# A two-layer encoder on one core: two moving operands in one 512-column matmul, and PSUM laid out anew

## The chip, the cores and the metric

The kernel runs on one core of a Trainium2 chip. The metric is the device time of one execution, in microseconds (us). Before the change three runs took 979.34, 980.66 and 981.9 us; the median is 980.66. A profile is one further execution, recorded by the hardware. Its rows name TensorE's products PE and its weight loads PEld, VectorE DVE, ScalarE ACT, GpSimd POOL and the engine that issues most transfers SP.

## What is computed

Two layers, each with three blocks on x (256 tokens by 1024, float32). The first and the third are feed-forwards, the second mixes tokens in three ways. Cut to what the change touches:

```python
def swiglu(x, w_gate, w_up, w_down):
    return (jax.nn.silu(x @ w_gate) * (x @ w_up)) @ w_down

for l in range(DEPTH):                                    # DEPTH = 2, D_FF = 2816
    x = layer_norm(ALPHA * x + 0.5 * swiglu(x, ffn1_w_gate[l], ffn1_w_up[l], ffn1_w_down[l]), ...)
    proj = x @ w_in[l]                                    # 1024 x 2560
    u, gb, gc, h, q, k, v = jnp.split(proj, splits, axis=-1)
    y_a = pool_mixer(u, pool_w[l], pool_scale[l])
    y_b = gated_conv_mixer(gb, gc, h, conv_w[l])
    y_c = neighbourhood_attention(q, k, v, rpb[l])        # 8 heads of 64
    x = layer_norm(ALPHA * x + jnp.concatenate([y_a, y_b, y_c], axis=-1) @ w_out[l], ...)
    x = layer_norm(ALPHA * x + 0.5 * swiglu(x, ffn2_w_gate[l], ffn2_w_up[l], ffn2_w_down[l]), ...)
```

## The kernel before

**Two parts of a number.** TensorE works here in a reduced float32 format (float32r). The kernel keeps precision by splitting each weight w into an upper part (whi, a cast on ScalarE, L178) and a lower part (wlo, the remainder, a subtraction on VectorE, L179), and each activation likewise: xhi and xlo (L270, L271), hT and yT with two halves. A product x w is then three matrix products: upper by upper, lower x by upper w, upper x by lower w.

**Units of weights.** All weights come in 330 units of 128 x 1024 (512 KB). `load` issues a unit's transfer on SP into one of 4 raw buffers and orders the two splits. 12 units may be live in split form. `Pacer` is a hand-written order: every group of products ends with `pc.step(us)`, which moves a planned clock on, runs the hooks that are due (work of other engines, and small TensorE jobs such as transposes, ordered with `pc.at(delay, tag, fn)`) and orders at most one further unit. `pc.need(tag)` runs the hooks of a tag at once. Each engine carries out its instructions in the order in which they were written.

**Three kinds of groups.**
- `x_stat` (L274 to L292): one tile of 128 tokens is stationary, 512 columns of weights move past; the result has tokens on its rows.
- `w_stat` (L294 to L309): 256 columns of weights are stationary, in two halves of 128 (`ft`), and all 256 tokens move past; the result comes transposed. For each half and each of the 8 chunks of 128 rows there are the three products L303, L304, L305 of 256 columns, all into one 256-column half of a bank. Two units and 48 products make a projection.
- `r_stat` (L311 to L317): activations stationary, 512 columns of weights moving, into the accumulators `acc`.

**Feed-forward.** The first four column tiles go through `x_stat`. Then, for each pair p of column tiles (2 to 10), `w_stat` makes gate; silu reads it from PSUM on ScalarE (L391); `w_stat` makes up; VectorE multiplies it by 0.5 and by silu's result into hf (L396); ScalarE and VectorE split hf into hT (L474, L475). The down projection of the pair before follows (24 products); those of the last three pairs are done in `finish`, one token tile after the other, with the layer norm, whose new x is transposed (L268) and split for the next block.

**Mixers.** v and the pair u, gb go through `x_stat`; q, k (two halves of the heads), gc and h through `w_stat`, in the order q0, k0, q1, k1, gc, h. The copies qT (L759, four with mirrored columns and the scale) and kT (L763) are read by the attention, whose steps are hooks: scores on TensorE (L686), bias and maximum on VectorE (L695, L697), exponentials on ScalarE (L700), normalisation on VectorE (L710, L712, tile pz), transposes of pz on TensorE (L721) that ScalarE copies out as PT (L726), and the products PT by v (L735, called PV below), copied out and split as yT. Two such stages (j = 0, 1) run for each half q of the heads. The pool mixer ends in a product of its own (L619, hook `ya`, 16 us on the planned clock after its means were ordered), the convolution runs on VectorE.

**PSUM** has 8 banks of 128 x 512 float32. `bank("acc")` takes one of 4 for the accumulators and the scores, `bank()` one of 4 others (tag `mm`) for everything else, in turn.

Of the kernel before, what the change touches and what calls it, by code (L numbers as in the profile page):

```python
# [9 lines left out]
F32 = mybir.dt.float32  # L10
# [50 lines left out]
# about how long a product of the tensor engine takes: these pace the work of the other engines  # L61
MM512 = 0.218
MM256 = 0.1095


class Pacer:
    """Places work of the other engines, and the next weights, between groups of matrix products."""
# [53 lines left out]
def encoder_kernel(  # L121
# [18 lines left out]
    ps_acc = ctx.enter_context(tc.tile_pool(name="ps_acc", bufs=4, space=PSUM))  # L140
    ps_mm = ctx.enter_context(tc.tile_pool(name="ps_mm", bufs=4, space=PSUM))
# [24 lines left out]
    def bank(tag="mm"):  # L166
        pool = ps_mm if tag == "mm" else ps_acc
        return pool.tile([P, 512], F32, tag=tag, name=nm(tag))

# [88 lines left out]
    def new_xT():  # L258
        hi = xp.tile([P, KC, SEQ], F32R, tag="xhi", name=nm("xhi"))
        lo = xp.tile([P, KC, SEQ], F32R, tag="xlo", name=nm("xlo"))  # L260
        return hi, lo
# [12 lines left out]
    def x_stat(ps, key, cols, t, xT, free):  # L274
        """One token tile against columns of the weights, a step per unit."""
# [18 lines left out]
    def w_stat(ps, key, xT):  # L294
        """256 columns of the weights against all tokens, transposed out."""
        for ft in range(2):
            c = slice(ft * P, (ft + 1) * P)
            for i in range(2):
                hi, lo = pc.get((*key, i))
                for j in range(4):  # L300
                    kc = i * 4 + j
                    o = ps[:, ft * SEQ : (ft + 1) * SEQ]
                    PE.matmul(o, hi[:, j, c], xT[0][:, kc, :], start=(kc == 0), stop=False)  # L303
                    PE.matmul(o, hi[:, j, c], xT[1][:, kc, :], start=False, stop=False)  # L304
                    PE.matmul(o, lo[:, j, c], xT[0][:, kc, :], start=False, stop=(kc == KC - 1))  # L305
                if ft == 1:
                    pc.free((*key, i))
                if ft == 0 or i == 0:
                    pc.step(12 * MM256)  # L309

    def r_stat(ps, key, act, t, n, first, last):  # L311
        """A chunk of transposed activations against half a row unit."""
# [86 lines left out]
    def ffn(key, xT, next_gb, stop, store=False):  # L399
# [17 lines left out]
        # first four column tiles with the token tiles apart  # L417
        gk, uk = (*key, "g", 0), (*key, "u", 0)
        if key == (0, 0):
# [9 lines left out]
            for k in (gk, uk):  # L429
                ps = [bank() for _ in range(NT)]  # L430
# [16 lines left out]
        else:  # L447
            for t in range(NT):
                pc.need(f"x{t}")
                gate = bank()  # L450
# [3 lines left out]
                up = bank()  # L454
# [10 lines left out]
        for p in range(2, NPAIR):  # L465
            gate = bank()
            w_stat(gate, (*key, "g", p), xT)
            sg = silu(gate)
            pc.step(12 * MM256)
            up = bank()  # L470
# [3 lines left out]
            ACT.copy(hT[:, 0], hf)  # L474
            DVE.tensor_tensor(hT[:, 1], hf, f32(hT[:, 0]), ALU.subtract)  # L475
            pc.step(12 * MM256)
            pc.need("h")
            # the down projection runs behind
# [15 lines left out]
    consts = {}  # L494

    def setup():
# [8 lines left out]
        # additive mask of a query column block: its rows run with the column falling  # L505
# [38 lines left out]
        pc.at(30, "cw", columns)  # L544
        # the bias table, each line in the middle of a longer one
# [12 lines left out]
        # probabilities: the columns out of a block's reach stay zero  # L558
# [26 lines left out]
    def mixers(l, xT, next_gb, stop):  # L585
# [12 lines left out]
        biases = {0: load_bias(l, 0)}  # L598

# [30 lines left out]
        for t in range(NT):  # L630
            pc.need(f"x{t}")
            pv = bank()
# [3 lines left out]
            pu = bank()  # L636
# [16 lines left out]
        def proj(name):  # L653
            ps = bank()
            w_stat(ps, (*key, name), xT)
            return ps.rearrange("p (a b) -> p a b", a=2)
# [13 lines left out]
        def attention(j, qT, kT, q):  # L670
            """Two heads, in the upper and the lower half of the rows: one stage after the other."""
# [174 lines left out]
```

## Time and profile before

| | |
|---|---|
| median of three runs (lowest, highest) | 980.66 us (979.34, 981.9) |
| profiled execution, from its first to its last instruction | 979.4 us |
| TensorE products | 6201, 4032 of them L303 to L305 |
| weight casts L178, weight splits L179 | 321 each, 1045 and 1231 ns |
| HBM read | 176.84 MB, 182 GB/s over the span |
| mean granted clock of TensorE | 0.991 |

The profile has only the span of the profiled execution; what lies before its first and after its last instruction isn't in it. A page of the profile gives shares of busy time, a chain that is followed back from the last instruction, and groups of instructions (line, engine, operation, written tile <- read tiles, shapes, count; then busy us, mean ns of one; then the engine's idle time before them and what ended it). A timeline gives start and duration of each instruction in us. Products are pipelined: a product's duration overlaps that of the next one.

### The profile page before, as it was taken

To read this page: it belongs to the slowest core of one execution; us is meant where nothing else is said; L and a number is where in the kernel's file an instruction comes from. 1 tells how busy PE (TensorE), PEld (TensorE's weight loads), DVE (VectorE), ACT (ScalarE), POOL (GpSimd) and SP (SyncE) were. 2 spreads that over 40 slices of the span, in tenths; PEclk is the share of its full clock that TensorE was granted. 3 is DMA by queue.
4 is the path that set the end of the run, shared out by engine and by line. 5 is a ranking of instruction groups with operands and counts; after the bars stand their busy time and mean duration, and the time that the engine had idled before them with its cause. 6 is when DMAs were issued, how large, how long until landed. Compare 5 with 4: busy or idle time off the path is not lost.

```text
span 979.4 us, 15259 instructions
## 1 busy us (share of the span) xinstructions
PE 950.6 (97%) x6201; PEld 865.1 (88%) x6201; DVE 580.3 (59%) x670; ACT 437.7 (45%) x585; POOL 65.6 (7%) x118
## 2 busy tenths in 40 slices
PE   7999999998999999999999999999889999999996
PEld 5999999878888999999888999998688889999995
DVE  5755544676768644545676454548676776454525
ACT  6544434335734534434344444443465354344410
POOL 4000000024101000000000000002050000000001
PEclk9999999999999999999999999999989999999999
DMA  8887665568345866565468556664754377556601
GB/s 287 277 264 216 190 194 173 145 185 241 106 129 169 258 194 188 175 195 177 135 211 254 176 172 194 191 186 110 252 153 123 109 229 243 177 174 193 192 23 43
DMA packets 129077, 178.95 MB, mean 183 GB/s; under 512 B 14752, under 2 KB 100848, under 8 KB 129008
## 3 DMA queue, kind: packets, MB, share of 16 engines
q1 hardware_dynamic: 129008, 177.99, 59.3%
q8 instruction: 48, 0.79, 0.3%
q14 instruction: 21, 0.17, 0.0%
HBM read 176.84 MB, written 1.13 MB: 182 GB/s over the span
## 4 chain that ended last, share of the span: by engine, by line
PE 83%; DVE 7%; DMA 5%; issue 2%; ACT 1%; POOL 1%; SPq 1%; POOLq 0%; DVEq 0%; ACTq 0%
PE mm L303 16%; PE mm L304 16%; PE mm L305 16%; PE acc L315 9%; PE acc L316 9%; PE acc L317 9%; DMA raw<-in_w_in_dram 3%; DVE wlo L179 2%; PE mm L292 2%; PE mm L290 2%; PE mm L291 2%; ACT whi L178 1%; PE mm L721 1%; DMA raw<-in_ffn_w_down_dram 1%; DMA raw<-in_ffn_w_up_dram 1%
## 5 line engine op out<-in xcount | busy, mean ns | idle before, releaser
L179 DVE TENSOR_TENSOR wlo<-raw,whi 128x1024 fp32r<-128x1024 f32 (+1 forms) x321 | 390.0, 1231 | 303.1 <-ACT whi L178 302.0
L178 ACT CAST whi<-raw 128x1024 fp32r<-128x1024 f32 (+1 forms) x321 | 331.1, 1045 | 328.9 <-issue 131.2
L303 PE MATMUL mm<-xhi,whi 128*128 128x256 f32 x1344 | 384.0, 286 | 0.0
L304 PE MATMUL mm<-xlo,whi 128*128 128x256 f32 x1344 | 382.0, 284 | 0.0
L305 PE MATMUL mm<-xhi,wlo 128*128 128x256 f32 x1344 | 381.8, 284 | 0.0
L303 PEld LDWEIGHTS mm<-xhi,whi 128*128 128x128 f32 x1344 | 259.7, 193 | 3.0 <-issue 1.5
L304 PEld LDWEIGHTS mm<-xlo,whi 128*128 128x128 f32 x1344 | 259.6, 193 | 1.4
L305 PEld LDWEIGHTS mm<-xhi,wlo 128*128 128x128 f32 x1344 | 259.5, 193 | 0.0
L315 PE MATMUL acc<-whi,hT 128*128 128x512 f32 x352 | 137.9, 392 | 0.0
L316 PE MATMUL acc<-whi,hT 128*128 128x512 f32 x352 | 137.4, 390 | 0.0
L317 PE MATMUL acc<-wlo,hT 128*128 128x512 f32 x352 | 137.0, 389 | 0.0
L317 PEld LDWEIGHTS acc<-wlo,hT 128*128 128x128 f32 x352 | 66.1, 188 | 14.0
L291 PE MATMUL mm<-whi,xlo 128*128 128x512 f32 x192 | 75.3, 392 | 2.9 <-DVE xlo L271 2.9
L315 PEld LDWEIGHTS acc<-whi,hT 128*128 128x128 f32 x352 | 66.2, 188 | 12.7
L316 PEld LDWEIGHTS acc<-whi,hT 128*128 128x128 f32 x352 | 66.2, 188 | 12.3
L290 PE MATMUL mm<-whi,xhi 128*128 128x512 f32 x192 | 76.7, 399 | 0.4 <-ACT whi L178 0.4
L292 PE MATMUL mm<-wlo,xhi 128*128 128x512 f32 x192 | 75.2, 392 | 0.5 <-DVE wlo L179 0.5
L342 POOL TENSOR_SCALAR rs<-mv 128x1 f32<-128x1 f32 x12 | 9.4, 780 | 847.0 <-DVE mv L341 847.0
L474 ACT CAST hT<-hf 128x512 fp32r<-128x512 f32 x36 | 22.3, 620 | 75.2 <-DVE hf L396 75.2
L291 PEld LDWEIGHTS mm<-whi,xlo 128*128 128x128 f32 x192 | 36.4, 189 | 10.8 <-DVE xlo L271 3.8
L292 PEld LDWEIGHTS mm<-wlo,xhi 128*128 128x128 f32 x192 | 36.2, 188 | 8.9 <-DVE wlo L179 1.3
L290 PEld LDWEIGHTS mm<-whi,xhi 128*128 128x128 f32 x192 | 36.3, 189 | 8.2 <-ACT whi L178 1.3
(93 smaller groups left out, 556.9 us busy)
## 6 DMA issues: line engine op xcount, KB each, us to landing
raw<-in_ffn_w_up_dram SPq DMA_DIRECT2D x88, 512.0 KB, 4.7
raw<-in_ffn_w_down_dram SPq DMA_DIRECT2D x88, 512.0 KB, 4.1
raw<-in_ffn_w_gate_dram SPq DMA_DIRECT2D x87, 512.0 KB, 4.1
raw<-in_w_in_dram SPq DMA_DIRECT2D x40, 512.0 KB, 4.7
raw<-in_w_out_dram SPq DMA_DIRECT2D x16, 512.0 KB, 4.8
lng<-in_ln_g_dram SPq DMA_DIRECT2D x6, 512.0 KB, 6.8
lnb<-in_ln_b_dram SPq DMA_DIRECT2D x6, 512.0 KB, 8.3
rbias<-tab SPq DMA_DIRECT2D x16, 96.0 KB, 5.1
```

What stands on the lines that cost most here:

```text
L178: ACT.copy(hi, raw)
L179: DVE.tensor_tensor(lo, raw, f32(hi), ALU.subtract)
L290: PE.matmul(ps, xT[0][:, kc, ts], hi[:, j, :], start=(kc == 0), stop=False)
L291: PE.matmul(ps, xT[1][:, kc, ts], hi[:, j, :], start=False, stop=False)
L292: PE.matmul(ps, xT[0][:, kc, ts], lo[:, j, :], start=False, stop=(kc == KC - 1))
L303: PE.matmul(o, hi[:, j, c], xT[0][:, kc, :], start=(kc == 0), stop=False)
L304: PE.matmul(o, hi[:, j, c], xT[1][:, kc, :], start=False, stop=False)
L305: PE.matmul(o, lo[:, j, c], xT[0][:, kc, :], start=False, stop=(kc == KC - 1))
L315: PE.matmul(ps, act[0][:, ts], hi[:, n, :], start=first, stop=False)
L316: PE.matmul(ps, act[1][:, ts], hi[:, n, :], start=False, stop=False)
L317: PE.matmul(ps, act[0][:, ts], lo[:, n, :], start=False, stop=last)
L474: ACT.copy(hT[:, 0], hf)
```

## The change

In `w_stat` the two products with the upper weights become one. xhi and xlo lie in one tile `xT` (2 x 8 x 256 columns a row); the moving operand is two runs of 256 columns, the upper and the lower part of the same chunk, and the 512 results fill a bank: upper by upper in its first half, lower x by upper w in its second. The product with the lower weights, 256 columns, goes on into the first half. The two halves are added when the result is read: `lower` copies the second halves of both banks to a tile in SBUF on ScalarE, and VectorE adds the first halves from PSUM.

A projection's result takes two banks. PSUM becomes one pool of 4 single banks, for accumulators, scores, and all transposes and small products, and one of 2 pairs of banks, for the results of `w_stat` and, as gate and up or v and u, of `x_stat`. As the out projection's accumulators take all four single banks, the attention of both halves (`a0`, `a1`) is asked for before it begins; `a1` was asked for 24 products later. The transpose that brings in the convolution's and the pool's scales (`columns`, hook `cw`) is ordered from the first mixers instead of the setup. The planned clock moves by 4 x 0.347 us for a quarter of a projection instead of 12 x 0.1095 us.

```diff
-MM256 = 0.1095
+MM768 = 0.347
-    ps_acc = ctx.enter_context(tc.tile_pool(name="ps_acc", bufs=4, space=PSUM))
-    ps_mm = ctx.enter_context(tc.tile_pool(name="ps_mm", bufs=4, space=PSUM))
+    ps_one = ctx.enter_context(tc.tile_pool(name="ps_one", bufs=4, space=PSUM))
+    ps_two = ctx.enter_context(tc.tile_pool(name="ps_two", bufs=2, space=PSUM))
...
+    def banks():
+        return ps_two.tile([P, 2, 2, SEQ], F32, tag="mm", name=nm("mm"))
...
     def new_xT():
-        hi = xp.tile([P, KC, SEQ], F32R, tag="xhi", name=nm("xhi"))
-        lo = xp.tile([P, KC, SEQ], F32R, tag="xlo", name=nm("xlo"))
-        return hi, lo
+        both = xp.tile([P, 2, KC, SEQ], F32R, tag="xT", name=nm("xT"))
+        return both[:, 0], both[:, 1], both
...
                     kc = i * 4 + j
-                    o = ps[:, ft * SEQ : (ft + 1) * SEQ]
-                    PE.matmul(o, hi[:, j, c], xT[0][:, kc, :], start=(kc == 0), stop=False)
-                    PE.matmul(o, hi[:, j, c], xT[1][:, kc, :], start=False, stop=False)
-                    PE.matmul(o, lo[:, j, c], xT[0][:, kc, :], start=False, stop=(kc == KC - 1))
+                    PE.matmul(
+                        ps[:, ft], hi[:, j, c], xT[2][:, :, kc, :],
+                        start=(kc == 0), stop=False, skip_group_check=True,
+                    )
+                    PE.matmul(
+                        ps[:, ft, 0], lo[:, j, c], xT[0][:, kc, :],
+                        start=False, stop=(kc == KC - 1), skip_group_check=True,
+                    )
                 if ft == 1:
                     pc.free((*key, i))
                 if ft == 0 or i == 0:
-                    pc.step(12 * MM256)
+                    pc.step(4 * MM768)
+
+    def lower(ps, scale=1.0):
+        t = tp.tile([P, 2, SEQ], F32, tag="t", name=nm("lw"))
+        ACT.activation(t, ps[:, :, 1], AF.Copy, scale=scale)
+        return t
...
-            gate = bank()
+            gate = banks()
             w_stat(gate, (*key, "g", p), xT)
-            sg = silu(gate)
-            pc.step(12 * MM256)
-            up = bank()
+            sg = lower(gate)
+            DVE.tensor_tensor(sg, gate[:, :, 0], sg, ALU.add)
+            ACT.activation(sg, sg, AF.Silu)
+            pc.step(4 * MM768)
+            up = banks()
             w_stat(up, (*key, "u", p), xT)
             hT = hts[p] = new_h()
-            hf = gated(up, sg).rearrange("p (a b) -> p a b", a=2)
+            hf = lower(up, 0.5)
+            DVE.scalar_tensor_tensor(hf, up[:, :, 0], 0.5, hf, ALU.mult, ALU.add)
+            DVE.tensor_tensor(hf, hf, sg, ALU.mult)
             ACT.copy(hT[:, 0], hf)
...
             pq = proj(f"q{q}")
+            ql = lower(pq, HD ** -0.5)
             qT = hp.tile([P, 2, 2, P], F32, tag="qk", bufs=4, name=nm("qT"))
+            DVE.scalar_tensor_tensor(ql, pq[:, :, 0], HD ** -0.5, ql, ALU.mult, ALU.add)
             for j in range(2):
                 for b in range(2):
-                    src = mirrored(pq[:, j, :].rearrange("p (r c) -> p r c", c=GRID)[:, :, b * QB : (b + 1) * QB])
-                    ACT.mul(qT[:, j, b, :].rearrange("p (r c) -> p r c", c=QB), src, HD ** -0.5)
+                    src = mirrored(ql[:, j, :].rearrange("p (r c) -> p r c", c=GRID)[:, :, b * QB : (b + 1) * QB])
+                    ACT.copy(qT[:, j, b, :].rearrange("p (r c) -> p r c", c=QB), src)
...
-            ACT.copy(kT, pk)
+            kl = lower(pk)
+            DVE.tensor_tensor(kT, pk[:, :, 0], kl, ALU.add)
...
-        pc.need("ya")
-        pc.need("a0")
+        for tag in ("ya", "a0", "a1"):
+            pc.need(tag)
```

gc and h are read in the same manner: `lower`, then a sum on VectorE.

**Where instructions stand, first place.** TensorE in a gate projection of the first feed-forward before; mm is its result, whi and wlo are the two parts of its two units, of which the rows show one chunk each.

```order
L303 MATMUL mm_874<-xhi_106,whi_601 128x256
L304 MATMUL mm_874<-xlo_107,whi_601 128x256
L305 MATMUL mm_874<-xhi_106,wlo_602 128x256
...
L303 MATMUL mm_874<-xhi_106,whi_624 128x256
L304 MATMUL mm_874<-xlo_107,whi_624 128x256
L305 MATMUL mm_874<-xhi_106,wlo_625 128x256
```

And after, the gate projection and the beginning of up, one chunk of each unit:

```order
L307 MATMUL mm_815<-xT_106,whi_572 128x512
L311 MATMUL mm_815<-xT_106,wlo_573 128x256
...
L307 MATMUL mm_815<-xT_106,whi_593 128x512
L311 MATMUL mm_815<-xT_106,wlo_594 128x256
...
L307 MATMUL mm_864<-xT_106,whi_615 128x512
L311 MATMUL mm_864<-xT_106,wlo_616 128x256
```

Three products of 256 columns have become one of 512 and one of 256, from one tile xT. 84 projections of 16 chunks and halves have 1344 fewer products.

**Second place.** TensorE in the mixers of layer 0, from the end of the first stage's transposes through the projection k1, before (L721 transposes of pz, L735 PV, L619 the pool product; the rows left out are further products of k1 and of PV):

```order
L721 MATMUL mm_2594<-ident,pz_598 128x128 x4
L303 MATMUL mm_2607<-xhi_1960,whi_2235 128x256
L304 MATMUL mm_2607<-xlo_1961,whi_2235 128x256
L305 MATMUL mm_2607<-xhi_1960,wlo_2236 128x256
...
L735 MATMUL mm_2632<-PT_2578,v_2088 64x256
L735 MATMUL mm_2632<-PT_2585,v_2088 64x256
...
L619 MATMUL mm_2651<-pT_2331,pw 128x256 x2
```

And after (L743, L757 and L641 in the same order):

```order
L743 MATMUL acc_2296<-ident,pz_561 128x128 x4
L307 MATMUL mm_2309<-xT_1702,whi_1978 128x512
L311 MATMUL mm_2309<-xT_1702,wlo_1979 128x256
...
L641 MATMUL acc_2318<-pT_2069,pw 128x256 x2
L307 MATMUL mm_2309<-xT_1702,whi_1991 128x512
...
L757 MATMUL acc_2335<-PT_2280,v_1829 64x256
L757 MATMUL acc_2335<-PT_2287,v_1829 64x256
```

Before, the pool product came behind PV, after two quarters of k1. Now it comes ahead of PV, after one quarter (four pairs), and its result, like the transposes' results, is one of the four single banks taken in turn.

**Third place.** ScalarE over the same stretch, before (qT reads the projection q1, mm_2453, in PSUM; PT the transposes):

```order
L178 CAST whi_2543<-raw_2542 128x1024
L759 ACTIVATE qT_2560<-mm_2453 128x128 x4
L726 COPY PT_2578<-mm_2573 128x512
L726 COPY PT_2585<-mm_2580 128x512
L726 COPY PT_2592<-mm_2587 128x512
L726 COPY PT_2599<-mm_2594 128x512
L178 CAST whi_2602<-raw_2601 128x1024
L748 CAST yT_2637<-mm_2632 128x4x32 x2
L748 CAST yT_2637<-mm_2642 128x4x32 x2
L623 ACTIVATE ya_2654<-mm_2651,cw 128x256 x2
```

And after (lw is the lower half of q1, L323 the copy in `lower`):

```order
L184 CAST whi_2246<-raw_2245 128x1024
L323 ACTIVATE lw_2259<-mm_2168 128x512
L783 COPY qT_2261<-lw_2259 128x128 x4
L748 COPY PT_2280<-acc_2275 128x512
L748 COPY PT_2287<-acc_2282 128x512
L748 COPY PT_2294<-acc_2289 128x512
L748 COPY PT_2301<-acc_2296 128x512
L184 CAST whi_2304<-raw_2303 128x1024
L645 ACTIVATE ya_2321<-acc_2318,cw 128x256 x2
L647 CAST yT_2324<-ya_2321 128x512
L770 CAST yT_2340<-acc_2335 128x4x32 x2
L770 CAST yT_2340<-acc_2345 128x4x32 x2
```

VectorE there, after: the end of the normalisation, a weight split, and the sum for q that qT waits for.

```order
L734 TENSOR_SCALAR pz_559<-pz_559,sm_2207 128x4x40 x2
L732 RECIPROCAL sm_2214<-sm_2214 128x2
L734 TENSOR_SCALAR pz_561<-pz_561,sm_2214 128x4x40 x2
L185 TENSOR_TENSOR wlo_2247<-raw_2245,whi_2246 128x1024
L779 SCALAR_TENSOR_TENSOR lw_2259<-mm_2168,lw_2259 128x512
L185 TENSOR_TENSOR wlo_2305<-raw_2303,whi_2304 128x1024
L648 TENSOR_TENSOR yT_2324<-ya_2321,yT_2324 128x512
```

Ahead of PT now stand a copy of the lower half and four copies of qT that wait for VectorE's sum, which stands behind the normalisation and one weight split.

More of the change, by code (lines that the diff above doesn't have):

```diff
@@ L164, in halves, with bank, apart @@
         return [slice(i * n // 2, (i + 1) * n // 2) for i in range(2)]
-    def bank(tag="mm"):
-        pool = ps_mm if tag == "mm" else ps_acc
-        return pool.tile([P, 512], F32, tag=tag, name=nm(tag))
+    def bank(tag="acc"):
+        return ps_one.tile([P, 512], F32, tag="acc", name=nm(tag))
+    def banks():
+        return ps_two.tile([P, 2, 2, SEQ], F32, tag="mm", name=nm("mm"))
+    def apart(two):
+        return two.rearrange("p a b c -> p a (b c)")
     def unit_tiles(shape):
@@ L428, in ffn @@
             res = []
-            for k in (gk, uk):
-                ps = [bank() for _ in range(NT)]
+            both = [apart(banks()) for _ in range(NT)]
+            for which, k in enumerate((gk, uk)):
+                ps = [b[:, which] for b in both]
                 seq = [(i, t) for i in range(4) for t in range(NT)]
@@ L449, in ffn @@
                 pc.need(f"x{t}")
-                gate = bank()
+                both = apart(banks())
+                gate, up = both[:, 0], both[:, 1]
                 x_stat(gate, gk, 512, t, xT, t == 1)
@@ L465, in ffn @@
         for p in range(2, NPAIR):
-            gate = bank()
+            gate = banks()
             w_stat(gate, (*key, "g", p), xT)
-            sg = silu(gate)
-            pc.step(12 * MM256)
-            up = bank()
+            sg = lower(gate)
[3 more added lines that the diff above has]
+            up = banks()
             w_stat(up, (*key, "u", p), xT)
             hT = hts[p] = new_h()
-            hf = gated(up, sg).rearrange("p (a b) -> p a b", a=2)
+            hf = lower(up, 0.5)
+            DVE.scalar_tensor_tensor(hf, up[:, :, 0], 0.5, hf, ALU.mult, ALU.add)
+            DVE.tensor_tensor(hf, hf, sg, ALU.mult)
             ACT.copy(hT[:, 0], hf)
             DVE.tensor_tensor(hT[:, 1], hf, f32(hT[:, 0]), ALU.subtract)
-            pc.step(12 * MM256)
+            pc.step(4 * MM768)
             pc.need("h")
@@ L542, in columns @@
             DVE.tensor_copy(cw, trp)
-        pc.at(30, "cw", columns)
+        consts["columns"] = columns
         tab = ap_.tile([P, 7 * TABW], F32, tag="a", name="tab")
@@ L598, in mixers @@
         biases = {0: load_bias(l, 0)}
+        if l == 0:
+            pc.at(POOL_AT - 4, "cw", consts["columns"])
         def pool_means():
@@ L631, in mixers @@
             pc.need(f"x{t}")
-            pv = bank()
+            both = apart(banks())
+            pv, pu = both[:, 0], both[:, 1]
             x_stat(pv, (*key, "v"), 512, t, xT, t == 1)
@@ L635, in mixers @@
             pc.step(6 * MM512)
-            pu = bank()
             x_stat(pu, (*key, "ug"), 512, t, xT, t == 1)
@@ L653, in proj @@
         def proj(name):
-            ps = bank()
+            ps = banks()
             w_stat(ps, (*key, name), xT)
-            return ps.rearrange("p (a b) -> p a b", a=2)
+            return ps
         def conv_mixer(z):
@@ L767, in qk @@
             pc.at(A_S + A_STEP, f"a{q}", second)
-            pc.step(12 * MM256)
+            pc.step(4 * MM768)
         qk(0)
@@ L774, in mixers @@
         gc = ap_.tile([P, 2, SEQ], F32, tag="a", name=nm("gc"))
-        ACT.copy(gc, p_)
-        pc.step(12 * MM256)
+        gl = lower(p_)
+        DVE.tensor_tensor(gc, p_[:, :, 0], gl, ALU.add)
+        pc.step(4 * MM768)
         p_ = proj("h")
+        hl = lower(p_)
         z = ap_.tile([P, 2, SEQ + 2], F32, tag="a", name=nm("z"))
@@ L780, in mixers @@
         POOL.memset(z[:, :, SEQ + 1 :], 0.0)
-        DVE.tensor_tensor(z[:, :, 1 : SEQ + 1], p_, gc, ALU.mult)
+        DVE.tensor_tensor(hl, p_[:, :, 0], hl, ALU.add)
+        DVE.tensor_tensor(z[:, :, 1 : SEQ + 1], hl, gc, ALU.mult)
         conv_mixer(z)
-        pc.step(12 * MM256)
+        pc.step(4 * MM768)
         acc = [[None, None], [None, None]]
@@ L802, in mixers @@
                 pc.step(6 * MM512)
-        pc.need("a1")
         return finish(keys[2:], act, acc, keys[-1], next_gb, False, stop)
```

2 lines of the change are left out of this document (1 added, 1 removed).

## The prediction

> **What bounds the kernel now.** I read the shares of the page first, then the chain that ended last, then who TensorE waited for.
>
> ```profile
> span 979.4 us, 15259 instructions
> PE 950.6 (97%) x6201; PEld 865.1 (88%) x6201; DVE 580.3 (59%) x670; ACT 437.7 (45%) x585; POOL 65.6 (7%) x118
> ...
> PE 83%; DVE 7%; DMA 5%; issue 2%; ACT 1%; POOL 1%; SPq 1%; POOLq 0%; DVEq 0%; ACTq 0%
> ```
>
> TensorE is busy for 97% of the span and holds 83% of the chain. A busy share alone doesn't prove a bound, so the next view is its own list of waits (in total, times, longest):
>
> ```profile
> PE mm L644 <- ACT un L639: 6.2, 2, 3.2
> PE mm L268 <- DMA x<-in_x_dram: 4.8, 2, 3.6
> PE mm L721 <- DVE pz L712: 4.6, 4, 1.4
> ```
>
> These three are 15.6 us; they stand at the start and in the mixers. In the feed-forward stages a window of 80 us shows none (columns: length, PE, PEld, DVE, ACT, POOL busy, clock, DMA share, GB/s), and the groups in it show how loaded the two engines are that will get more work:
>
> ```profile
> 100.00:180.00 80.00, 80.00 (x583) 76.17 (x582) 40.44 (x38) 34.54 (x39) 0.00 (x0) 1.00 0.62 185
> ```
> ```profile
> L179 DVE TENSOR_TENSOR wlo<-raw,whi 128x1024 fp32r<-128x1024 f32 x28 | 34.0, 1225 | 35.6 <-ACT whi L178 35.6
> L475 DVE TENSOR_TENSOR hT<-hf,hT 128x512 fp32r<-128x512 f32 x5 | 3.5, 694 | 3.4 <-ACT hT L474 3.4
> L396 DVE SCALAR_TENSOR_TENSOR hf<-mm,sg 128x512 f32<-128x512 f32 x5 | 3.4, 684 | 0.0
> ```
> ```profile
> L178 ACT CAST whi<-raw 128x1024 fp32r<-128x1024 f32 x29 | 29.9, 1045 | 36.4 <-issue 22.9 <-PE mm L304 13.5
> L474 ACT CAST hT<-hf 128x512 fp32r<-128x512 f32 x5 | 3.1, 621 | 9.5 <-DVE hf L396 9.5
> L391 ACT ACTIVATE sg<-mm 128x512 f32<-128x512 f32 x5 | 3.0, 597 | 2.3 <-PE mm L305 2.3
> ```
>
> TensorE is busy for all 80 us while VectorE works 40.44 and ScalarE 34.54. So in these stages time is what one product after another takes.
>
> **Term 1: the products.** A product's own duration overlaps the next, so what it costs is the distance from start to start. The timeline of TensorE around one down projection (columns: start us, duration) gives it for both lengths and both change-overs. At its start,
>
> ```profile
> 564.06 0.28 PE L303 MATMUL mm<-xhi,whi 128*128 128x256 f32 x1
> 564.18 0.28 PE L304 MATMUL mm<-xlo,whi 128*128 128x256 f32 x1
> 564.30 0.28 PE L305 MATMUL mm<-xhi,wlo 128*128 128x256 f32 x1
> 564.42 0.40 PE L315 MATMUL acc<-whi,hT 128*128 128x512 f32 x1
> ```
>
> once it is steady,
>
> ```profile
> 565.81 0.39 PE L315 MATMUL acc<-whi,hT 128*128 128x512 f32 x1
> ```
>
> at its end,
>
> ```profile
> 569.66 0.39 PE L317 MATMUL acc<-wlo,hT 128*128 128x512 f32 x1
> 569.89 0.28 PE L303 MATMUL mm<-xhi,whi 128*128 128x256 f32 x1
> ```
>
> and at the start of the next:
>
> ```profile
> 581.40 0.40 PE L315 MATMUL acc<-whi,hT 128*128 128x512 f32 x1
> ```
>
> - From 569.89 to 581.40 stand 96 products of 256 columns (two projections): 11.51 / 96 = 119.9 ns each, a triple 359.7 ns.
> - From 565.81 to 569.89 stand 18 products of 512 columns: 4.08 / 18 = 226.7 ns each.
> - At the change-overs a 256 before a 512 takes 0.12 (564.30 to 564.42) and a 512 before a 256 takes 0.23 (569.66 to 569.89): the order of lengths costs nothing.
>
> 256 more columns cost 226.7 - 119.9 = 106.8 ns, so 13.1 ns of each product don't depend on its length. The change makes a pair of each triple: 226.7 + 119.9 = 346.6 ns, 13.1 ns less.
>
> ```profile
> L303 PE MATMUL mm<-xhi,whi 128*128 128x256 f32 x1344 | 384.0, 286 | 0.0
> ```
>
> There are 1344 triples (84 projections of 16): 1344 x 13.1 = **17.6 us** less.
>
> No row shows a moving operand in two runs of 256 columns, or this mixture in one accumulation. The upper bound is that the 512 costs what its two halves do now, 239.8 ns, and nothing is saved; the lower is 17.6, as the rows above deny that mixing shortens anything. I take 17.6, since the rows of 512 columns are nearest. With the average over the whole down projection (564.42 to 569.89, 24 products, 227.9) it is 16.0.
>
> The Trainium skill, "TensorE: Matmul & The Clock Gate", section "Wait — 56ns, not 53.3ns?", gives a warm product N / 2.4 GHz plus about 2.5 ns: by it the removed product is worth 1344 x 2.5 = 3.4 us, an estimate from that page. The trace disagrees: 119.9 and 226.7 ns leave some 13 ns beside the streaming, not 2.5.
>
> **Term 2: more work for ScalarE and VectorE.** Each projection's result comes in two PSUM halves. ScalarE copies the lower ones out, VectorE adds the upper. The nearest rows are L391 (597 ns, PSUM to SBUF) and L396 (684 ns, PSUM and SBUF in). In a feed-forward pair of 17 us that is two `lower` of 0.6 on ScalarE, and on VectorE two operations more (the sum of gate; the product with sg, no longer part of hf), 1.4 us. In the 80 us above (five pairs) ScalarE goes to some 41 us and VectorE to some 47: both stay far below TensorE, which hides them. ScalarE now also waits between `lower` and silu for VectorE's sum, and the weight casts are queued behind that. A cast that starts 2 us later is harmless as long as up to 12 units are live and one is used every 2.8 us (17 / 6). PSUM gives no wait: gate and up take turns in two pairs of banks, and each has a whole projection (5.5 us) to be emptied.
>
> Only the **last pair** of a feed-forward has a deadline. Its down projection comes 18 products after its up projection ends (12 for two chunks in both halves of the columns, 6 for two more chunks in one half): 18 x 226.7 = 4.1 us. Now, after another pair:
>
> ```profile
> 565.32 0.68 DVE L396 SCALAR_TENSOR_TENSOR hf<-mm,sg 128x512 f32<-128x512 f32 x1
> 566.69 0.69 DVE L475 TENSOR_TENSOR hT<-hf,hT 128x512 fp32r<-128x512 f32 x1 [0.69 <-ACT hT L474]
> ```
>
> hf starts 0.9 us after the projection (564.42) and the low part is there at 567.38, 2.96 us after. The change puts a `lower` (0.6) and one more VectorE operation (0.69) into that: 4.3 us, against 4.1 + 0.23 for the product that needs it. I count 0.3 us for all four feed-forwards; if VectorE is in a weight split just then, 1.2 each.
>
> **Term 3: the mixers**, where chains are short of time already. First attention stage, layer 0: TensorE, VectorE, ScalarE.
>
> ```profile
> 247.96 0.30 PE L721 MATMUL mm<-ident,pz 128*128 128x128 f32 x1 [0.87 <-DVE pz L712]
> 249.44 2.42 PE L721 MATMUL mm<-ident,pz 128*128 128x128 f32 x15 [1.18 <-DVE pz L712]
> ```
> ```profile
> 251.60 0.36 PE L303 MATMUL mm<-xhi,whi 128*128 128x256 f32 x1
> ```
> ```profile
> 250.73 0.52 DVE L712 TENSOR_SCALAR pz<-pz,sm 128x160 f32<-128x160 f32 x2
> 251.16 1.22 DVE L179 TENSOR_TENSOR wlo<-raw,whi 128x1024 fp32r<-128x1024 f32 x1
> ```
> ```profile
> 249.46 0.75 ACT L759 ACTIVATE qT<-mm 128x128 f32<-128x128 f32 x4
> 250.11 2.42 ACT L726 COPY PT<-mm 128x512 f32<-128x512 f32 x4
> ```
>
> - **The copies PT.** Now ScalarE writes qT from PSUM and goes on to PT at 250.11. After the change it must wait for VectorE to sum q, and that stands behind the normalisation and a weight split: 251.16 + 1.22 = 252.4, sum 0.7, four qT copies 0.75, first PT 0.6: 254.4. The pool product (now L619, after the attention's PV) has moved ahead of PV and shares four banks with everything here: its bank is that of the first PT. TensorE reaches it four pairs after 251.60, at 253.0, and waits **1.5 us**; PV behind it then finds the other PTs done. In layer 1 TensorE runs at half clock there (below), 16 products take twice as long, and the wait disappears: 0. Bounds: 0 to 1.5 each; I take 1.5 in all.
> - **The scores.** kT gets VectorE's sum behind a split. With k ending at 0: `lower` done at 0.8, split done at 0.9 to 1.05, sum 0.7, so kT at 1.75; TensorE asks for it at 1.39 + 0.2 (four pairs). 0.2 us four times (two stages, two layers): 0.8. Bounds 0 to a whole split (1.2) each.
> - **The softmax** takes as long as before and TensorE comes 0.3 us sooner (12 pairs save 0.16, and some delay of kT): the waits for pz grow by 0.3 four times: 1.2.
>
> Sum of term 3: 3.5 us, and with the 0.3 of term 2 **3.8 us**.
>
> A wait can also cost clock:
>
> ```profile
> 251.60:258.40 6.80, 6.80 (x55) 5.74 (x54) 3.12 (x6) 3.53 (x9) 0.00 (x0) 1.00 0.53 154
> 721.40:729.20 7.80, 6.07 (x53) 5.53 (x53) 7.48 (x12) 6.13 (x21) 3.48 (x3) 1.00 0.56 177
> 729.20:736.00 6.80, 5.96 (x28) 5.96 (x29) 4.52 (x12) 3.86 (x9) 0.69 (x3) 0.50 0.26 75
> ```
>
> (columns as in the window above). In layer 1 the same stage, with the same waits, was followed by 6.8 us at half clock; in layer 0 it wasn't. The scores of the first and the second stage start, in layer 0 and in layer 1 (timeline; the last row is from the chain in order of time), at
>
> ```profile
> 241.23 1.36 PE L686 MATMUL acc<-kT,qT 64*128 64x160 f32 x16
> ```
> ```profile
> 261.88 1.36 PE L686 MATMUL acc<-kT,qT 64*128 64x160 f32 x16
> ```
> ```profile
> 721.31 1.36 PE L686 MATMUL acc<-kT,qT 64*128 64x160 f32 x16
> ```
> ```profile
> 744.76 1.29 PE acc L686 x16
> ```
>
> 20.65 us apart in layer 0 and 23.45 in layer 1: the stretch cost 2.8 us.
>
> The Trainium skill, "TensorE: Matmul & The Clock Gate", section "What's actually happening", has the clock halved after an idle window of about 3.4 us, windows that run free of the kernel: the trace agrees in the size (clock 0.50 for 6.8 us, two such windows), and by that rule it is chance whether layer 0 falls into it. I leave the forecast at one such stretch, as now, and keep 2.8 us either way for the range.
>
> **Sum.** 979.4 - 17.6 + 3.8 = 965.6 for the span. The profile shows no time outside the span; the median of the three runs is 980.66 and the lowest 979.34, so the profiled one lies 1.3 us under the median. On the median: 980.66 - 13.8 = **967 us**, 1.4% faster.
>
> **Rivals.**
> - *The waits are hidden:* banks and sums come in time and only term 1 counts: 980.7 - 17.6 = 963. For it: the feed-forwards hold 72 of the 84 projections and have no waits. Against: the PT chain above has no slack. 15%.
> - *The mixers cost more:* a whole split in front of each kT (4 x 1.2), a wait for the pool product in layer 1 too (1.5) and a half-clock stretch in layer 0 (2.8) come to 9.1 on top of 3.8, less the 0.8 counted for the scores: 980.7 - 17.6 + 12.1 = 975. 13%.
> - *Slower: the two-run product costs two products.* Place: the moving operand of each upper product (the upper part of x and, 2048 columns on, the lower). If its second run costs a start of its own, it takes 239.8 instead of 226.7, term 1 is 0 and the 3.8 stay: 984.5. From 226.7 + 13.1 - 3.8 / 1.344 = 237 ns on, the change loses. Against: start-to-start differs by 106.8 ns for 256 columns, so the columns stream and the start is per instruction. 8%.
> - *The pair keeps most of the 13.1 ns*, because they hang on the change from upper to lower weights and back, which stays, and not on the product that goes. If that leaves a fifth of term 1, 3.5 us, the 3.8 eat it: 981. Against: from 564.06 to 564.18 the weights are the same, and it takes 0.12 as the others do. 3%. The 2.5 ns of the Trainium skill ("TensorE: Matmul & The Clock Gate", "Wait — 56ns, not 53.3ns?") would come to the same 3.4 us.
> - *It doesn't do what it says:* the feed-forward isn't bound by TensorE once triples are pairs, because casts held up behind the sums starve it by the 0.42 us that each pair of projections saves (32 x 13.1 ns): the 36 pairs then give back 15.1, and 982 results. Against: ScalarE's 36.4 us of idle time before its 29 casts. 5%.
>
> Forecast 56%, its own range 965 to 970. The range should leave out the slow rivals alone: 960 (all waits hidden and layer 1's stretch gone) to 977. About 0.3% (3 us) is what a measurement of this kernel can tell from no change: faster 0.84, same 0.08, slower 0.08.
>
> **What would show it.** Term 1: products of the new lines with 0.35 us from one upper product to the next, and TensorE's count down by 1344. Term 2: a feed-forward window with TensorE still busy throughout, VectorE at about 60%. Term 3: in the list of TensorE's waits the pool product waiting for the first PT copy or kT's sum with 1 to 2 us each. The prediction is wrong if the pair takes more than 0.355, if TensorE waits for casts or splits in the feed-forward, or if the clock row of the mixers holds more stretches below 1.

## The result and the profile after

The changed kernel takes **996.05 us** (median of four runs, 991.53 to 998.67), the kernel before 981.28 beside it: 1.0151 times as long, 95% interval 1.0118 to 1.0184. The forecast was 967, its range 960 to 977. The sign was wrong and the range missed.

The page of the profiled execution after (998.49 us; its span, the busy shares, the chain that ended last):

```profile
span 996.7 us, 12739 instructions
PE 953.0 (96%) x4857; PEld 795.8 (80%) x4857; DVE 632.7 (63%) x754; ACT 484.8 (49%) x663; POOL 65.0 (7%) x118
...
PE 82%; DVE 7%; DMA 5%; ACT 2%; issue 2%; POOL 1%; SPq 1%; POOLq 0%; DVEq 0%; ACTq 0%
```

TensorE has 1344 products fewer, as planned, is still busy for 96%, and yet the span is 17.3 us longer. A busy share of 96% hid the loss, so the next view is TensorE's list of waits (in total, times, longest):

```profile
PE mm L295 <- ACT sg L406: 11.6, 7, 3.2
PE mm L295 <- ACT v L657: 8.2, 4, 3.5
PE acc L273 <- DMA x<-in_x_dram: 5.3, 2, 3.6
PE acc L743 <- DVE pz L734: 4.1, 4, 1.2
PE mm L307 <- DVE hf L411: 3.1, 1, 3.1
PE acc L641 <- issue: 1.4, 2, 1.2
PE mm L296 <- DVE xT L276: 1.2, 2, 0.6
PE acc L708 <- DVE kT L788: 0.5, 2, 0.3
```

They sum to 35.4 us. The same list before has 20.5 in seven rows, the three of the prediction and these:

```profile
PE mm L291 <- DVE xlo L271: 2.9, 2, 1.5
PE mm L408 <- DVE hf L396: 1.1, 2, 0.9
PE mm L292 <- DVE wlo L179: 0.5, 1, 0.5
PE mm L290 <- ACT whi L178: 0.4, 1, 0.4
```

Two rows are new after the change, and they are the largest: L295, the first of the three products in `x_stat`, waits for ScalarE's silu (sg) in the feed-forwards and for the copy of v in the mixers. It doesn't need either as an input. (A third new row, L307 behind hf, stands there once: a `w_stat` result takes over a pair of banks, and its first product, which goes into the first bank, waits until VectorE has read `up` from the second.) The timeline shows one of these places, the first feed-forward of layer 1 (start, duration, in brackets the idle time before and what ended it):

```profile
518.62 1.04 ACT L184 CAST whi<-raw 128x1024 fp32r<-128x1024 f32 x1 [1.73 <-DMA raw<-in_ffn_w_down_dram]
519.58 0.59 ACT L406 ACTIVATE sg<-mm 128x512 f32<-128x512 f32 x1
```
```profile
520.22 0.80 PE L295 MATMUL mm<-whi,xT 128*128 128x512 f32 x1 [3.20 <-ACT sg L406]
520.81 0.63 PE L296 MATMUL mm<-whi,xT 128*128 128x512 f32 x1
```

and the same place before:

```profile
508.15 1.05 ACT L178 CAST whi<-raw 128x1024 fp32r<-128x1024 f32 x1 [1.66 <-DMA raw<-in_ffn_w_down_dram]
...
509.11 0.59 ACT L391 ACTIVATE sg<-mm 128x512 f32<-128x512 f32 x1
509.19 0.39 PE L290 MATMUL mm<-whi,xhi 128*128 128x512 f32 x1
```

In both kernels silu of gate stands on ScalarE behind a weight cast that waits for a transfer, and is late. Before, TensorE runs through it at its usual pace (0.39 us for each product). After, the first product of `up` stands still until silu has read gate, and what follows takes 0.63 instead of 0.39. In two windows (columns: length, PE, PEld, DVE, ACT, POOL busy, clock, DMA share, GB/s) after,

```profile
100.00:180.00 80.00, 80.00 (x427) 68.37 (x426) 47.56 (x50) 41.05 (x50) 0.00 (x0) 1.00 0.59 184
518.00:526.80 8.80, 6.58 (x16) 5.18 (x17) 4.04 (x4) 4.56 (x5) 0.00 (x0) 0.61 0.72 206
```

and one before at the same place:

```profile
505.00:515.00 10.00, 10.00 (x59) 8.78 (x57) 6.34 (x7) 5.97 (x8) 0.00 (x0) 1.00 0.85 268
```

the granted clock is 0.61 on average around the wait, and it falls during it, at 519.5:

```profile
516.10:519.51 3.41, 0.92 (x4) 0.39 (x3) 0.81 (x2) 1.26 (x2) 0.00 (x0) 1.00 0.95 325
519.51:526.33 6.82, 6.11 (x14) 4.81 (x15) 3.67 (x3) 3.60 (x5) 0.00 (x0) 0.50 0.66 181
```

Over the whole span the clock is 0.982 after and 0.991 before; times the spans, 17.9 and 8.8 us of full clock are missing. 14.9 us more of waits and 9.1 of clock are 24 us, of which something must have been won back for 17.3 to remain. (This adds up only roughly: a clock that is low while TensorE stands still costs nothing.) The Trainium skill, "TensorE: Matmul & The Clock Gate", section "What's actually happening", has the clock halved after an idle window of about 3.4 us and given back after a busy one. The trace agrees in the length: the clock was at half for 6.8 us, two such windows. It doesn't agree that the window must be idle: in the 3.41 us before the fall TensorE was busy for 0.92.

What was won is in the products (groups by line: busy, mean ns of one; then two starts eight pairs apart):

```profile
L307 PE MATMUL mm<-xT,whi 128*128 128x512 f32 x1344 | 478.6, 400 | 3.1 <-DVE hf L411 3.1
L311 PE MATMUL mm<-xT,wlo 128*128 128x256 f32 x1344 | 377.2, 281 | 0.0
```
```profile
99.74 0.40 PE L307 MATMUL mm<-xT,whi 128*128 128x512 f32 x1
...
102.56 0.40 PE L307 MATMUL mm<-xT,whi 128*128 128x512 f32 x1
```

2.82 us for eight pairs are 352.5 ns a pair, where 346.6 were forecast and a triple took 359.7. (Over all 1344 pairs of the trace the medians are 236 ns after a 512 and 117 after a 256, 353 together.) So two things went wrong: a wait that wasn't in the sum, and a saving of 7 ns in place of 13.

### The profile page after: what moved, and what is told of

Read it like the earlier page. It is cut to its first block, busy times and chain, and to the rows that moved or that the text cites. A ratio compares the mean times of both kernels' runs of the same rounds, so it can differ in the third digit from the quotient of the medians.

```text
span 996.7 us, 12739 instructions
## 1 busy us (share of the span) xinstructions
PE 953.0 (96%) x4857; PEld 795.8 (80%) x4857; DVE 632.7 (63%) x754; ACT 484.8 (49%) x663; POOL 65.0 (7%) x118
## 4 chain that ended last, share of the span: by engine, by line
PE 82%; DVE 7%; DMA 5%; ACT 2%; issue 2%; POOL 1%; SPq 1%; POOLq 0%; DVEq 0%; ACTq 0%
PE mm L307 30%; PE mm L311 15%; PE acc L330 9%; PE acc L332 9%; PE acc L331 9%; PE mm L295 3%; DVE wlo L185 2%; PE mm L296 2%; PE mm L297 2%; DMA raw<-in_w_in_dram 2%; DMA raw<-in_ffn_w_down_dram 2%; ACT whi L184 1%; PE acc L743 1%; DMA raw<-in_ffn_w_up_dram 1%; DVE x L362 1%
## 5 line engine op out<-in xcount | busy, mean ns | idle before, releaser
L307 PE MATMUL mm<-xT,whi 128*128 128x512 f32 x1344 | 478.6, 400 | 3.1 <-DVE hf L411 3.1
L311 PE MATMUL mm<-xT,wlo 128*128 128x256 f32 x1344 | 377.2, 281 | 0.0
L307 PEld LDWEIGHTS mm<-xT,whi 128*128 128x128 f32 x1344 | 252.6, 188 | 67.0 <-issue 5.7
L311 PEld LDWEIGHTS mm<-xT,wlo 128*128 128x128 f32 x1344 | 253.9, 189 | 1.3
L295 PE MATMUL mm<-whi,xT 128*128 128x512 f32 x192 | 82.8, 431 | 19.8 <-ACT sg L406 11.6
L296 PE MATMUL mm<-whi,xT 128*128 128x512 f32 x192 | 80.2, 418 | 1.2 <-DVE xT L276 1.2
L297 PE MATMUL mm<-wlo,xT 128*128 128x512 f32 x192 | 79.6, 415 | 0.1
L323 ACT ACTIVATE lw<-mm 128x512 f32<-128x512 f32 x84 | 50.3, 598 | 40.1 <-PE mm L311 39.9
L295 PEld LDWEIGHTS mm<-whi,xT 128*128 128x128 f32 x192 | 38.9, 203 | 32.9 <-ACT sg L406 14.6
L297 PEld LDWEIGHTS mm<-wlo,xT 128*128 128x128 f32 x192 | 39.0, 203 | 9.9 <-DVE wlo L185 1.1
L296 PEld LDWEIGHTS mm<-whi,xT 128*128 128x128 f32 x192 | 39.1, 204 | 9.5 <-DVE xT L276 2.0
L495 DVE TENSOR_TENSOR hT<-lw,hT 128x512 fp32r<-128x512 f32 x36 | 24.9, 693 | 24.7 <-ACT hT L494 24.7
```

The costliest lines, as they stand in the source:

```text
L295: PE.matmul(ps, xT[0][:, kc, ts], hi[:, j, :], start=(kc == 0), stop=False)
L296: PE.matmul(ps, xT[1][:, kc, ts], hi[:, j, :], start=False, stop=False)
L297: PE.matmul(ps, xT[0][:, kc, ts], lo[:, j, :], start=False, stop=(kc == KC - 1))
L307: PE.matmul(ps[:, ft], hi[:, j, c], xT[2][:, :, kc, :], start=(kc == 0), stop=False, skip_group_check=True,)
L311: PE.matmul(ps[:, ft, 0], lo[:, j, c], xT[0][:, kc, :], start=False, stop=(kc == KC - 1), skip_group_check=True,)
L323: ACT.activation(t, ps[:, :, 1], AF.Copy, scale=scale)
```

## The experiments

**Theory A:** `gate` and `up` of one token tile (v and u in the mixers) now lie in one two-bank PSUM tile, and the program orders the first write into the tile's second bank behind the read of its first, which it doesn't touch. The lost time is this wait and the half clock behind it. **B:** it is the new sums on ScalarE and VectorE, or the four banks that everything in the mixers shares. **C:** it is the 512-column product with two runs.

**Crossing the halves.** Only which result lies in which tile is changed (likewise for v and u, and in the first feed-forward); `apart` gives a view of a tile by its two banks. The tiles are still shared, but between the last product of one token tile's gate and the next write into its tile now lie the 24 products of its `up`, some 5.4 us, in which silu can read:

```
+            both = [apart(banks()) for _ in range(2)]
             for t in range(NT):
-                both = apart(banks())
-                gate, up = both[:, 0], both[:, 1]
+                gate, up = both[0][:, t], both[1][:, t]
```

> The changed kernel with the results of the two token tiles crossed: both gates share one two-bank tile, both ups the other (in the mixers both v and both u). Theory A, the changed kernel's loss is TensorE's wait at the first product of up or u for ScalarE's read of gate or v, because both lie in one PSUM tile, with the half-clock stretches behind those waits: the 11.6 and 8.2 us of waits of the x-stationary line on ScalarE and the 3.1 us for hf go, the clock is back at 0.99 or 1.00 there, and the time falls from 996 by some 25 to 32 us, to 964 to 971. Theory B, the loss comes from the sums on ScalarE and VectorE or from the four banks that everything in the mixers shares: within 3 us of 996. Theory C, the loss comes from the two-run product of 512 columns: within 3 us of 996.

Measured: 974.37 us, 0.9935 [0.9911, 0.996] of the kernel before. The waits of this kernel:

```profile
PE acc L666 <- ACT un L661: 5.6, 2, 3.1
PE acc L273 <- DMA x<-in_x_dram: 4.6, 2, 3.7
PE acc L743 <- DVE pz L734: 3.7, 4, 1.2
PE acc L423 <- DVE hf L411: 3.0, 4, 1.2
PE mm L296 <- DVE xT L276: 2.9, 2, 1.5
PE acc L641 <- issue: 2.5, 2, 1.2
PE acc L708 <- DVE kT L788: 0.9, 2, 0.7
```

and the same place in its timeline, where silu is as late as ever and TensorE doesn't care:

```profile
503.40 0.40 PE L295 MATMUL mm<-whi,xT 128*128 128x512 f32 x1
...
504.77 1.05 ACT L184 CAST whi<-raw 128x1024 fp32r<-128x1024 f32 x1 [1.33 <-DMA raw<-in_ffn_w_down_dram]
...
505.46 0.39 PE L295 MATMUL mm<-whi,xT 128*128 128x512 f32 x1
505.68 0.39 PE L296 MATMUL mm<-whi,xT 128*128 128x512 f32 x1
505.72 0.59 ACT L406 ACTIVATE sg<-mm 128x512 f32<-128x512 f32 x1
```

The first row is the first product of `up`: it starts 2.3 us before silu reads gate. The same instructions, durations and operands, 22 us less. B and C fall as the cause. A had said 25 to 32, and was too high: it took all 22.9 us of the three rows away, but other waits grew. That for un (the copy of u and gb, which L666 transposes) is 5.6 us and had no row in the changed kernel, xT went from 1.2 to 2.9, the pool product (L641) from 1.4 to 2.5. The two spans differ by 23.4 us; TensorE's waits by 11.4 (35.4 and 24.0, with two rows of 0.5 and 0.3 not shown), and its clock, in the rows of the cores,

```profile
core 0: 996.7 us, clock 0.982
```
```profile
core 0: 973.3 us, clock 0.994
```

by 17.9 - 5.8 = 12.1 us. By this reckoning, for these two executions, the half clock cost as much as the waits. In the changed kernel's trace it stands in six stretches before the last products, 30.7 us together, and five of them begin during a wait for sg or v or within 1.5 us behind it; the crossed kernel has one, of 6.8 us. The share isn't the same in each execution: the four runs of the changed kernel were granted 0.982 to 0.992, and the one with 0.992 still took 991.53 us.

**The layout alone**, the other way round: the new PSUM tiles, but three products of 256 into one half, and no sums.

```
-                    PE.matmul(
-                        ps[:, ft], hi[:, j, c], xT[2][:, :, kc, :],
...
+                    o = ps[:, ft, 0]
+                    PE.matmul(o, hi[:, j, c], xT[0][:, kc, :], start=(kc == 0), stop=False)
+                    PE.matmul(o, hi[:, j, c], xT[1][:, kc, :], start=False, stop=False)
+                    PE.matmul(o, lo[:, j, c], xT[0][:, kc, :], start=False, stop=(kc == KC - 1))
...
-            sg = lower(gate)
-            DVE.tensor_tensor(sg, gate[:, :, 0], sg, ALU.add)
-            ACT.activation(sg, sg, AF.Silu)
+            sg = tp.tile([P, 2, SEQ], F32, tag="t", name=nm("sg"))
+            ACT.activation(sg, gate[:, :, 0], AF.Silu)
```

> The PSUM layout and order of the changed kernel alone: three products of 256 columns into one half as before, no lower half and no sums. Theory A: the waits of the x-stationary line on ScalarE (some 20 us) and the half clock behind them are there as in the changed kernel, and the pair's 13 us are not saved: 1005 to 1013. Theory B (the sums) or C (the two-run product): neither is in it, so 978 to 985, as before.

Measured: 998.16 us, 1.0186 [1.0155, 1.0217]. Two of its waits:

```profile
PE mm L295 <- ACT sg L402: 8.9, 6, 2.0
PE mm L295 <- ACT v L651: 8.4, 4, 3.5
```

The loss comes with the tiles alone, by 7 us less than A said. Some 5 us of this are the pairs, which A took at 13 us and which are worth 7.8 (below); and the waits for sg are 2.7 us shorter here.

**Crossed in the feed-forwards only:** the edit above without its mixer part.

> The changed kernel with the results crossed in the four feed-forwards only; in the two mixers v and u of one token tile still share a PSUM tile. Theory A, each wait costs where it stands, with the clock behind it: the 8.2 us of waits for v stay and those for sg go, and the time lies between the crossed kernel (974) and the changed one (996), at 982 to 988. If the waits in one of the two stages are hidden anyway, it comes out at 974 (the mixers' wait costs nothing) or at 996 (the feed-forwards' costs nothing), within 3 us.

Measured: 977.62 us, 0.9973 [0.9954, 0.9991]; a miss, for A and for both alternatives. The start of its list of waits:

```profile
PE mm L295 <- ACT v L657: 7.0, 4, 3.1
PE acc L273 <- DMA x<-in_x_dram: 5.2, 2, 3.7
PE acc L743 <- DVE pz L734: 4.0, 4, 1.2
```

The wait for v is there with 7.0 us, but that for un (5.6 in the crossed kernel, 6.2 before) isn't: in the mixers TensorE already waited for ScalarE a little later, and mostly does it earlier now. Shared tiles there cost some 3.7 us, to about 3 (0.9973 against 0.9935, each to 0.002 or 0.0025); the other 18 (996.05 - 977.62) are the feed-forwards', where TensorE hadn't waited for silu at all.

**The pair against its two halves.** The crossed kernel, the 512-column product split again. In this kernel a start in one half of a bank makes the first chunk's upper product drop out of the sum of the other half; the instructions and their order are those of a full sum.

```
-                    PE.matmul(
-                        ps[:, ft], hi[:, j, c], xT[2][:, :, kc, :],
-                        start=(kc == 0), stop=False, skip_group_check=True,
-                    )
+                    for part in range(2):
+                        PE.matmul(
+                            ps[:, ft, part], hi[:, j, c], xT[part][:, kc, :],
+                            start=(kc == 0), stop=False, skip_group_check=True,
+                        )
```

> The crossed kernel, with each product of 512 columns split again into two of 256 into the same two PSUM halves: all layout, sums and order of the change without the fewer products. If the pair saves what the starts in the changed kernel say, 1344 x (359.7 - 353.5) = 8 us by the medians to 13 us by the means, it is 8 to 13 us slower than the crossed kernel. If the pair saves the forecast 17.6 us, it is 17 to 18 us slower. If a two-run product costs its two halves, both are the same within 2 us.

Measured: 982.15 us, 1.0024 [1.0005, 1.0044]. So the pairs are worth 7.8 us in the crossed kernel (to about 3, by the two intervals), just under the 8 to 13 of the starts and not 17.6. And this kernel against the one before is the price of everything else, the sums, the new layout and the mixers' order: 2.4 us, with an interval of 0.5 to 4.3.

**The sums alone:** the crossed kernel with each result read from its upper half as before, the lower one left unread.

```
-            sg = lower(gate)
-            DVE.tensor_tensor(sg, gate[:, :, 0], sg, ALU.add)
-            ACT.activation(sg, sg, AF.Silu)
+            sg = tp.tile([P, 2, SEQ], F32, tag="t", name=nm("sg"))
+            ACT.activation(sg, gate[:, :, 0], AF.Silu)
...
```

> The crossed kernel without what the second PSUM half costs ScalarE and VectorE: the lower halves are computed but not read, and each result leaves PSUM as in the kernel before (the product of x's lower part is left out of the result). If the sums cost what the prediction counted in its terms 2 and 3, it is 3 to 4 us faster than the crossed kernel; if they cost what split products with sums cost over the kernel before, 2 us; if they are wholly hidden, 0.

Measured: 972.79 us, 0.9926 [0.9899, 0.9953], 1.6 us under the crossed kernel's 974.37 on another chip, with intervals that overlap widely. The sums cost little; how little isn't settled.

**One run in place of two.** A chunk's upper and lower x lie next to each other:

```
-        both = xp.tile([P, 2, KC, SEQ], F32R, tag="xT", name=nm("xT"))
-        return both[:, 0], both[:, 1], both
+        both = xp.tile([P, KC, 2, SEQ], F32R, tag="xT", name=nm("xT"))
+        return both[:, :, 0], both[:, :, 1], both
...
-                        ps[:, ft], hi[:, j, c], xT[2][:, :, kc, :],
+                        ps[:, ft], hi[:, j, c], xT[2][:, kc],
```

> The crossed kernel, with the upper and lower part of a chunk of x next to each other, so that the 512 moving columns are one run. The products of 512 columns in a projection take 236 to 237 ns from start to start in the changed kernel, against 226.7 in the down projections. If the second run costs the difference, they fall to 227 and the time falls by 1344 x 9 to 10 ns = 12 to 13 us below the crossed kernel, to 952 to 959. If the difference comes from alternating between 512 and 256 columns or between upper and lower weights, both kernels take the same within 2 us.

Measured: 973.0 us, 0.9927 [0.9902, 0.9952]. Two starts in it, eight pairs apart:

```profile
106.73 0.40 PE L307 MATMUL mm<-xT,whi 128*128 128x512 f32 x1
```
```profile
109.56 0.40 PE L307 MATMUL mm<-xT,whi 128*128 128x512 f32 x1
```

2.83 us, 353.8 ns a pair as with two runs; over all pairs the medians are again 236 and 117 ns. The second run costs nothing.

**The order of lengths.** What is left is the alternation of 512 and 256. The prediction's own rows had held a sign: from 564.42 to 565.81 six products of 512 behind a row of 256 take 231.7 ns each, not 226.7. First 16 of the one, then 16 of the other (`units_` holds the projection's two units):

```
         for ft in range(2):
             c = slice(ft * P, (ft + 1) * P)
+            for kc in range(KC):
+                PE.matmul(
+                    ps[:, ft], units_[kc // 4][0][:, kc % 4, c], xT[2][:, :, kc, :],
...
+        for ft in range(2):
+            c = slice(ft * P, (ft + 1) * P)
+            for kc in range(KC):
+                PE.matmul(
+                    ps[:, ft, 0], units_[kc // 4][1][:, kc % 4, c], xT[0][:, kc, :],
```

> The crossed kernel with the products of a projection in another order: first all 16 of 512 columns, then all 16 of 256. One run of the crossed kernel shows 236 ns after a product of 512 and 117 after one of 256 in strict alternation. Theory D, alternation itself costs: in the kernel before, the first five products of 512 after a row of 256 take 233, 236, 228, 233 and 231 ns instead of 227, so 26 ns more, and the first two of 256 after a row of 512 take 113 and 119, so 8 ns less; one change each way per 16 pairs then costs 18 ns in place of 16 x 6.5. The starts go to 227 and 120, and the time falls by 84 x (16 x 6.5 - 18) ns = 7 us, to 966 to 969. If the two kinds of product cost 236 and 117 in any order, the time stays within 2 us of the crossed kernel.

Measured: 968.76 us, 0.9902 [0.9871, 0.9933]. One row of 16, not behind a change of length, up to the next:

```profile
121.89 3.79 PE L305 MATMUL mm<-xT,whi 128*128 128x512 f32 x16
125.51 0.76 PE L314 MATMUL mm<-xT,wlo 128*128 128x256 f32 x5
```

3.62 / 16 = 226.3 ns each: the same product, the same two runs, at the down projection's pace. Over the whole kernel the medians are 227 and 120 ns. As the first comparison with the crossed kernel was across two chips, both ran once more on one.

> The crossed kernel once more, on one chip with the rows of 16: 0.9935 of the kernel before, if it comes out as it did (971 to 977).

> The kernel with rows of 16 once more, beside the crossed one. If alternation costs what the starts say (238.5 and 117.4 ns in the crossed kernel, 231.1 and 120.0 in rows of 16, 4.8 ns for each of 1344 pairs), it is 6 to 7 us below the crossed kernel on this chip, at 0.986 to 0.990 of the kernel before; if the 5.6 us between their first runs were the difference of two chips, within 2 us of it.

Measured: 973.66 us and **968.08 us**, 0.9934 [0.9907, 0.996] and 0.9876 [0.9843, 0.9909]: again 5.6 us apart, a little under the 6 to 7 that D gave. D holds, and this version beats both kernels. A change-over after every 4 chunks came beside the first run of 16:

> As the kernel with rows of 16, but the two kinds of product change over after every 4. Theory D: 4 pairs take 4 x 346.6 + 18 ns or less in place of 4 x 353, so the kernel gains 84 x 4 x 8 ns = 2.6 us on the crossed one, a third of what rows of 16 gain. If the order does not matter, within 2 us of the crossed kernel.

Measured: 970.16 us, 0.9912 [0.9879, 0.9945], between the two; its interval holds the first results of both.

## Why the prediction was wrong

- **The step that failed** is in term 2: "PSUM gives no wait: gate and up take turns in two pairs of banks, and each has a whole projection (5.5 us) to be emptied." That is so for the pairs p = 2 to 10 of `w_stat`, and the window from 100 to 180 us shows it. It isn't for the first four column tiles and for v and u: there the diff gives gate and up the two banks of one tile, `up` is written straight after gate's last product, and the time to empty gate is nothing. The prediction priced the edits of `w_stat` and of the mixers' projections and passed over the edit in `ffn` and `mixers` that looked like mere naming. In its place the runs showed 22 us (996.05 against 974.37 with the halves crossed), in the profiled executions about half of it waits and half the clock behind them. None of the prediction's signs of being wrong named such a wait.
- **Term 1** had the right sign and the wrong size: 17.6 us forecast, 7.8 measured by splitting the products again, 8 to 10 by the starts (1344 x 359.7 less 353.8 or 352.5). The step was "the order of lengths costs nothing", read from the one distance at each change-over. The cost comes in the next five; the prediction saw the 227.9 ns average of that stretch, and gave it as 1.6 us, as if it came once in a down projection and not with every pair. With 16 in a row 5.6 us of it are won.
- **Terms 2 and 3** can stand in their sum: 3.8 us forecast, 2.4 [0.5, 4.3] measured. VectorE and ScalarE are at 47.56 and 41.05 us in the window, as worked out (47 and 41). Of the mixers' waits, the one for the pool product (L641) is 1.4 us where 1.5 were forecast (its row names no releaser; that it waits for the first PT copy is not shown) and the one for kT 0.5 in place of 0.8; that for pz didn't grow (4.6 before, 4.1 after), where 1.2 us more were forecast.
- **The half clock** was kept "at one such stretch, as now". The trace before already has three, two of 3.4 us (from 227.4 and 708.7) beside the one of 6.8; the changed kernel has six. Waits and clock aren't independent: the missed waits cost about as much again in clock here (12.1 us beside 11.4). It isn't a fixed rate: the layout alone waits 17.3 us for sg and v, against 19.8, and has a clock of 0.989.
- **From span to median** the prediction put the profiled execution 1.3 us under the median. Spans lie 1.8 us under the times here (996.7 and 998.49, 973.3 and 975.08), so it was rather 0.5 over. The forecast doesn't hang on it, as the 13.8 us were taken from the median.
- **The slow rivals.** That of the two-run product has the right side by luck: its mechanism, the second run, costs nothing, and a pair takes 352.5 to 353.8 ns, about half way from the forecast's 346.6 to the rival's 359.7, where the change loses only from 237 + 119.9 = 357 on. The rival by which the pair keeps most of the 13.1 ns (3%) comes nearer in size, as somewhat over half is kept, but not in its mechanism: before, a product of 256 behind a change from upper to lower weights or back took 120 ns in the median, like one behind none. With the right price of the pair and no shared tile the time is that of the crossed kernel, 974: inside the range.

## What to carry to other kernels

When a tile is made larger, go through every place that gets two results into it, and ask of each write what must have read the other half first; a wait is set by the tile, not by the bytes. Look for it in the list of waits as an engine that waits for something it doesn't read. And take the price of an instruction from a stretch that has its neighbours too: one distance at a change-over doesn't show what the change-over costs.

## What the runs showed of the hardware

- A change of length costs TensorE later than at the change: products of 512 and 256 columns in strict turn take 352.5 to 353.8 ns a pair where rows of equal ones take 226.3 + 119.9 = 346.2 (medians over whole kernels: 236 + 117 in turn, 227 + 120 in rows of 16). What makes it so is open; that weights change from upper to lower at each step isn't enough, as the triples before changed them too at 119.9.
- A moving operand in two runs of 256 columns costs the same as one of 512: 352.5 and 353.8 ns a pair, 974.37 and 973.0 us on one chip.
- The clock needs no idle window to fall. In the traces here it falls as if at the ends of windows of 3.413 us that follow one another through an execution: the changed kernel's seven falls (222.55, 314.71, 519.51, 714.07, 744.79, 806.23 and 990.55 us) lie a whole number of them apart, to 0.01 us. The first six come behind windows in which TensorE was busy for 0.92 to 1.47 us, 27 to 43%. Cut into such windows, the twelve traces of this case show no fall behind more than 53% and, at full clock and after the first 3 us, none missing behind less than 44%. So a wait of 2 to 3.5 us costs clock in one execution and not in the next, by where the windows lie.
- A second start in a bank, while the other half's sum has begun, makes that half's next product overwrite and not add: the output of the kernel with split products is 0.112 (relative) away from the reference, and leaving the first chunk's upper product out of these projections in the reference changes it by 0.112 too. The Trainium skill, "PSUM — Partial Sum Buffer", section "The four PSUM rules", has this rule for two groups open in one bank; the run agrees.
